# Two decoder layers in one launch: gates and one gelu written through tanh

## The chip, the cores and the metric

The kernel runs on one core of one Trainium2 chip. The metric is the device time of one execution in microseconds. Three executions of the kernel before took 1547.25, 1549.53 and 1549.8 us; the median is 1549.53 us. In the text PE is TensorE, DVE is VectorE, ACT is ScalarE, POOL is GpSimd and SP is SyncE, which here only starts DMAs.

## The reference, cut to what matters

288 rows (256 of a prompt and 8 x 4 of samples) pass two layers with shared weights. Each layer is a half-step SwiGLU, a mixer, and a second half-step SwiGLU. The mixer is what changes:

```python
h = _rmsnorm(x, p['g_mix'])
u, v, q, k, vv, qi, ki, wi, ga, gb = jnp.split(h @ p['w_in'], SPLIT_POINTS, axis=-1)
u = jax.nn.gelu(u)                       # the tanh form is jax's default
v = _rmsnorm(jax.nn.gelu(v), p['g_v'])
...
sv, attn = mixer(v, q, k, vv, qi, ki, wi)
merged = sigmoid(ga) * ((u * sv) @ p['w_pa']) + sigmoid(gb) * (attn @ p['w_pb'])
x = x + merged @ p['w_out']
```

`sv` is a causal 128x128 mix of `v` per channel group plus a bias. `attn` is attention over keys that an indexer chose: 64 of the prompt's own keys, or 256 out of 2052 for a sample, whose keys and values lie in a paged cache. All is fp32.

## The kernel before, in words

The residual `x` stays in on-chip memory, transposed, as eight blocks of 128 features by 288 rows. All large products are *units* (`add_unit`): one weight tile of 128x1024 fp32 (512 KB) gives one PSUM tile `mm` of 128x288. To keep fp32 precision in the PE's fp32r mode, weights and activations are each split in a rounded high part and a low rest: `wh`, `wl` (`unit_split`, lines 487 to 506: ACT copies `raw` to `wh`, DVE subtracts to get `wl`) and blocks `b` by `Pair.add` and `Pair.put` (lines 582 to 597). A unit then is 8 times 3 matmuls: high x high, high x low, low x high. That makes 9840 matmuls into `mm`. The `raw` tiles have four buffers and are loaded by DMAs that ACT's queue starts once a split is written; the three `mm` tiles rotate.

A mixer has, in order, units for the index key and weight, `qi`, `q`, `k`, `v` of the attention, `v` of the gating, seven of `gb`, eight of `u`, then eight times a `ga` unit and a `w_pa` unit, the last `gb`, eight of `w_pb` and eight of `w_out`. Each ends in an evacuation (`ev_u`, `ev_ga`, ...), a generator that issues the ACT and DVE work on the PSUM tile. `ta`, `tb` and `tc` are scratch tiles with two buffers each.

Between the units the sparse attention runs as generators (`sample`, `sample_qk`, `two_heads`, `attend`, ...): small matmuls into PSUM tiles `s`, softmax on ACT (tiles `lg` for the prompt, `lgs` for the samples, both with `AF.Exp`) and DVE. The samples' paged keys (`in_kT`) and values (`in_cv`) come through four 1 MB tiles named `ring`: SP starts eight DMAs of 128 KB for each tile (`loader`, lines 681 to 710), and two tiles at a time are multiplied (`s<-ring,qz` for keys, `s<-ring,b` for values).

The order on each engine is fixed when the program is built. Every instruction passes through `Engine.__getattr__` (line 294, which is why nearly all rows carry that line), which adds an estimated duration to a model clock of that engine. Generators give up their turn until the model says their operands are there (`ready`, `go`), and PSUM tiles of the attention are granted by the same clocks. So a changed estimate changes the order. For ACT the model adds 1283 ns when an activation needs another table than the last one (`TABLES`, line 218); activations that are not in `TABLES` never change the model's table. The actual `ACT_TABLE_LOAD` instructions are put in by the compiler.

Of the kernel before, what the change touches and what calls it, by code (L numbers as in the profile page):

```python
# [9 lines left out]
F32 = mybir.dt.float32  # L10
# [3 lines left out]
AF = mybir.ActivationFunctionType  # L14
OP = mybir.AluOpType
# [14 lines left out]
T = SEQ + DB * DT  # L30
# [11 lines left out]
LW = 2052  # L42
NB = 67
RING = 4

O_ID, O_SW, O_SEL = 0, 128, 256
O_CM, O_WSM, O_WSS, O_WM, O_MN, O_HM, O_ER = 384, 768, 896, 928, 992, 1056, 1064
# [167 lines left out]


class Engine:
    TABLES = {AF.Exp: "exp", AF.Silu: "silu", AF.Gelu_apprx_tanh: "gelu", AF.Sigmoid: "sigmoid"}

    def __init__(self, clocks, name, engine):  # L220
        self.c, self.n, self.e, self.table, self.mode = clocks, name, engine, None, None
# [1 line left out]
    def cost(self, k, a, kw):  # L223
# [33 lines left out]
        if self.n == "S":  # L257
            psum = str(getattr(a[1], "space", "")).endswith("PSUM")
            w = (51 if psum else 93) + 0.833 * n + 93 * ("accum_out" in kw)
            w += 94 * (hasattr(kw.get("scale"), "ap") + hasattr(kw.get("bias"), "ap"))  # L260
            t = self.TABLES.get(a[2])
            if t and t != self.table:
# [42 lines left out]
def trunk(ctx, tc, A, OUT):  # L305
    nc = tc.nc
    V, S, P, Q, PE = nc.vector, nc.scalar, nc.gpsimd, nc.sync, nc.tensor
    clocks = Clocks()
    clk = clocks.t
    V, S, P, Q, PE = (Engine(clocks, n, e) for n, e in (("V", V), ("S", S), ("P", P), ("Q", Q), ("PE", PE)))  # L310
# [4 lines left out]
    hlp = ctx.enter_context(tc.tile_pool(name="hlp", bufs=3))  # L315
    rgp = ctx.enter_context(tc.tile_pool(name="rgp", bufs=RING))
    tp = ctx.enter_context(tc.tile_pool(name="tp", bufs=2))
# [21 lines left out]
    x = cp.tile([128, KT, T], F32, name="x")  # L339
# [51 lines left out]
    def spawn_front(g):  # L391
        gens.insert(0, ((-1, 1e9), g))
# [11 lines left out]
    def go(eng, *aps):  # L404

        for _ in range(PRM["turn_n"]):
            if hurry[0] or clocks.after(aps, by=eng) <= max(clk["PE"], clk[eng]) and clk[eng] <= clk["PE"] + PRM["turn"]:
                return
            yield
# [124 lines left out]
    def sumsq(n, src):  # L534
        while squares[0] != n:
            yield
        if n == 0:
            S.activation(acc[:, :T], src, AF.Square)
        else:
            q = tp.tile([128, T], F32, tag="sq", name="sq")  # L540
            S.activation(q, src, AF.Square)
            yield from go("V", q)
            V.tensor_tensor(acc[:, :T], acc[:, :T], q, op=OP.add)
        squares[0] = (n + 1) % KT
# [13 lines left out]
    def rms_gen(key, full=True):  # L558
        yield from ready(acc)
        ps, tag = yield from palloc()  # L560
        sums(ps, acc)
        rs = mp.tile([128, 3], F32, tag="rs", name="rs", bufs=2)
        ms = mp.tile([128, 3], F32, tag="ms", name="ms", bufs=2)
        V.tensor_scalar(ms, ps[:, :3], 1.0 / D, EPS, op0=OP.mult, op1=OP.add)
        pfree(tag)
        P.tensor_tensor(rs, ms, mhalf.to_broadcast([128, 3]), op=OP.pow)
        yield from ready(rs)
        ps, tag = yield from palloc()
        c0 = 0 if full else 256
        spread(ps, lambda j: rs[:, j:j + 1], full)  # L570
        rb = mp.tile([128, T], F32, tag="rb", name="rb", bufs=2)
        copy(rb[:, c0:], ps[:, c0:T])
        pfree(tag)
        rstd_now[key] = (rb, rs)

    class Pair:
# [11 lines left out]
            V.scalar_tensor_tensor(lo.t, t, g, h.t.bitcast(F32), op0=OP.mult, op1=OP.subtract)  # L588
            self.h[n], self.l[n] = h, lo

        def put(self, n, t):
            h, lo = Block(F32R), Block(F32R)
            yield from go("S", t)
            S.activation(h.t, t, AF.Copy)
            yield from go("V", h.t)
            V.tensor_tensor(lo.t, t, h.t.bitcast(F32), op=OP.subtract)
            self.h[n], self.l[n] = h, lo

        def __call__(self, k):
# [81 lines left out]
    def loader():  # L681
        yield from wait("idx")
        n = 0
        for key in want:
# [4 lines left out]
            else:  # L689
                while n - state["used"] >= RING:  # L690
                    yield
# [21 lines left out]
    def mixer(l, xp, key, nxt, next_gain, next_rms):  # L713
        M = {"q": [], "sq": [], "qi": [], "vg": {}, "sv": {}, "ma": {}, "sb": {}}
        xs, a_, t_, m_ = Pair(), Pair(), Pair(), Pair()
# [88 lines left out]
        def ev_u(n):  # L804
            def ev(ps):
                t = tp.tile([128, T], F32, tag="ta", name="ta")
                S.activation(t, ps[:, :T], AF.Gelu_apprx_tanh)
                yield from go("V", t)
                V.tensor_tensor(t, t, M["sv"][n].t, op=OP.mult)
                M["sv"][n].free()  # L810
                yield from a_.put(n, t)
            return ev

        def ev_ga(n):
            def ev(ps):
                t = M["sa", n] = tp.tile([128, T], F32, tag="ta", name="ta")
                S.activation(t, ps[:, :T], AF.Sigmoid)
                yield
            return ev

        def ev_pa(n):
            def ev(ps):
                b = Block()
                M["ma"][n] = b
                V.tensor_tensor(b.t, ps[:, :T], M.pop(("sa", n)), op=OP.mult)
                yield
            return ev

        def ev_gb(n):
            def ev(ps):  # L830
                b = Block()
                M["sb"][n] = b
                S.activation(b.t, ps[:, :T], AF.Sigmoid)
                yield
            return ev

        def ev_pb(n):
            def ev(ps):
                t = tp.tile([128, T], F32, tag="ta", name="ta")
                V.tensor_tensor(t, ps[:, :T], M["sb"][n].t, op=OP.mult)  # L840
                m = tp.tile([128, T], F32, tag="tb", name="tb")
                V.tensor_tensor(m, t, M["ma"][n].t, op=OP.add)
                M["sb"][n].free()
                M["ma"][n].free()
                yield from m_.put(n, m)
            return ev

        def ev_out(n):
            def ev(ps):
                V.tensor_tensor(x[:, n], ps[:, :T], x[:, n], op=OP.add)  # L850
                yield from nxt.add(n, next_gain(n))
                yield from sumsq(n, x[:, n])
                if n == KT - 1:
                    spawn_front(rms_gen(next_rms))
            return ev
# [6 lines left out]
        for nm in PRM["order"].split() + ["gb", "u"]:  # L862
            n, ev = evs_[nm]
# [725 lines left out]
    def idle(what):  # L1589
        n = 0  # L1590
        while not what():
            hurry[0] = True
            if n > 4:
                clk["PE"] += 200
            hook()
            evacs(True)
            n += 1
            assert n < 1000
        hurry[0] = False
        return n  # L1600
# [8 lines left out]
    for i, u in enumerate(units):  # L1609
# [3 lines left out]
        n = idle(lambda: u["need"] is None or u["need"] in flags)  # L1613
# [84 lines left out]
```

## Time and profile before

| | |
|---|---|
| median of three executions | 1549.53 us |
| the profiled execution | 1547.6 us |
| its span, first to last instruction | 1545.8 us |
| PE busy | 1515.0 us, 98% |
| DVE busy | 976.0 us, 63% |
| ACT busy | 768.6 us, 50%, of it 69.3 us in 54 table loads |
| moved by DMA | 299.75 MB, mean 194 GB/s |

A row of a group of instructions reads: line, engine, operation, tiles written <- tiles read, shape, count, then busy us and mean ns of one, then the idle time of the engine right before them and what ended it. PE's instructions overlap: a 128x288 matmul is shown with some 295 ns, but they start 0.13 us apart. A PE that is busy 98% has little time to give back: the 1.8 us between the span and the execution's time lie outside the program.

### The profile page before, as it was taken

The numbers are of one execution on the slowest core, as the hardware profiler recorded it, in microseconds if no ns is written. First come the engines' busy times: TensorE is split into PE (matmuls) and PEld (weight loads), VectorE is DVE, ScalarE is ACT, GpSimd is POOL, SyncE is SP. The second block draws the span as 40 slices with busy tenths as digits, with TensorE's granted clock in tenths as the row PEclk, the third lists the DMA queues.
The fourth block names the chain that finished last, engine by engine and source line by source line (L and its number), as shares of the span: only waits on it lengthen the run. The fifth ranks groups of instructions, "written<-read, shape, count | busy, mean of one in ns | idle before, by whom it ended". The sixth has DMA issues, their size and how long they took to land.

```text
span 1545.8 us, 32344 instructions
## 1 busy us (share of the span) xinstructions
PE 1515.0 (98%) x12110; PEld 1444.6 (93%) x12110; DVE 976.0 (63%) x1987; ACT 768.6 (50%) x1241; POOL 52.5 (3%) x65
## 2 busy tenths in 40 slices
PE   8999999999999999999999999999999999999999
PEld 7999998987879999999999999989887799999999
DVE  6666558875554666665556665588855547666643
ACT  5444444657773454444444444446578634544432
POOL 1000011100000000000000000201000000000000
PEclk9999999999999999999999999999999999999999
DMA  7666555587887665545545555556888854454563
GB/s 256 213 206 192 174 156 161 179 268 239 261 273 232 209 191 194 166 165 164 168 158 167 171 159 162 155 165 191 272 250 276 278 176 164 162 166 164 162 181 112
DMA packets 162558, 299.75 MB, mean 194 GB/s; under 512 B 21857, under 2 KB 108386, under 8 KB 162402
## 3 DMA queue, kind: packets, MB, share of 16 engines
q10 hardware_dynamic: 61552, 212.95, 43.0%
q1 hardware_dynamic: 100850, 84.73, 18.0%
q8 instruction: 97, 1.59, 0.4%
q14 instruction: 59, 0.48, 0.1%
HBM read 294.83 MB, written 2.77 MB: 193 GB/s over the span
## 4 chain that ended last, share of the span: by engine, by line
PE 77%; issue 14%; DMA 4%; ACT 2%; DVE 2%; SPq 1%; POOL 1%; POOLq 0%; DVEq 0%; ACTq 0%
PE mm L294 71%; PE s L294 6%; DMA raw<-in_win 1%; DMA ring<-in_kT 1%; DMA ring<-in_cv 1%; SPq L294 1%; ACT L294 1%; POOL rs L294 0%; DVE b L294 0%; DVE wl L294 0%; ACT b L294 0%; ACT wh L294 0%; DMA b<-in_ws 0%; DMA x<-in_x 0%; ACT lg L294 0%
## 5 line engine op out<-in xcount | busy, mean ns | idle before, releaser
L294 PE MATMUL mm<-b,wh 128*128 128x288 f32 x6560 | 1327.5, 298 | 4.8 <-DVE b L294 2.6
L294 PEld LDWEIGHTS mm<-b,wh 128*128 128x128 f32 x6560 | 1047.5, 188 | 24.4 <-issue 14.3
L294 PE MATMUL mm<-b,wl 128*128 128x288 f32 x3280 | 965.9, 294 | 2.3 <-DVE wl L294 1.6
L294 ACT ACTIVATE wh<-raw 128x1024 fp32r<-128x1024 f32 (+3 forms) x421 | 435.0, 1034 | 548.9 <-PE mm L294 538.9
L294 DVE TENSOR_TENSOR wl<-raw,wh 128x1024 fp32r<-128x1024 f32 (+3 forms) x421 | 503.2, 1197 | 264.4 <-ACT wh L294 259.7
L294 PEld LDWEIGHTS mm<-b,wl 128*128 128x128 f32 x3280 | 615.9, 188 | 3.5 <-DVE wl L294 3.5
L294 DVE TENSOR_TENSOR ta<-mm,rb 128x288 f32<-128x288 f32 x88 | 40.3, 458 | 55.6 <-PE mm L294 49.3
L294 ACT ACT_TABLE_LOAD x54 | 69.3, 1283 | 9.5 <-DMA ring<-in_cv 3.7
L294 DVE TENSOR_TENSOR tc<-mm,tb 128x288 f32<-128x288 f32 x88 | 40.3, 458 | 52.6 <-PE mm L294 52.2
L294 POOL TENSOR_TENSOR rs<-ms,mhalf 128x3 f32<-128x3 f32 x8 | 11.4, 1423 | 1111.2 <-DVE ms L294 1035.4
L294 DVE TENSOR_SCALAR_CACHE_REDUCE jk<-z,ci 128x513 bf16<-128x513 f32 x62 | 46.6, 751 | 2.2
L294 DVE TENSOR_TENSOR tb<-ta,rb 128x288 f32<-128x288 f32 x88 | 39.7, 452 | 4.9 <-ACT ta L294 4.9
L294 DVE TENSOR_TENSOR b<-tc,b 128x288 fp32r<-128x288 f32 x88 | 39.7, 451 | 0.0
L294 PE MATMUL s<-ring,qz 128*32 128x256 f32 x512 | 34.2, 383 | 4.4 <-DMA ring<-in_kT 4.4
L294 ACT ACTIVATE b<-tc 128x288 fp32r<-128x288 f32 x88 | 37.7, 429 | 1.5 <-DVE tc L294 1.0
L294 ACT ACTIVATE ta<-ta 128x288 f32<-128x288 f32 x88 | 37.8, 430 | 0.8 <-DVE ta L294 0.7
L294 ACT ACTIVATE jk<-z,ci 128x513 bf16<-128x513 f32 x30 | 21.8, 726 | 30.0 <-DVE ci L294 28.5
L294 PE MATMUL s<-ring,b 128*32 128x256 f32 x512 | 33.9, 382 | 2.5 <-DMA ring<-in_cv 2.5
L294 DVE SCALAR_TENSOR_TENSOR x<-mm,x 128x288 f32<-128x288 f32 x32 | 14.7, 458 | 31.4 <-PE mm L294 31.4
L294 PEld LDWEIGHTS s<-ring,qz 128*32 128x32 f32 x512 | 16.4, 109 | 16.5 <-issue 5.8
L294 PEld LDWEIGHTS s<-ring,b 128*32 128x32 f32 x512 | 16.7, 109 | 15.2 <-DMA ring<-in_cv 5.3
L294 ACT ACTIVATE b<-s 128x16 fp32r<-128x16 f32 (+2 forms) x62 | 16.4, 280 | 26.3 <-PE s L294 13.1
(193 smaller groups left out, 845.3 us busy)
## 6 DMA issues: line engine op xcount, KB each, us to landing
raw<-in_wup ACTq DMA_DIRECT2D x173, 512.0 KB, 3.5
raw<-in_win ACTq DMA_DIRECT2D x96, 512.0 KB, 4.3
ring<-in_kT SPq DMA_DIRECT2D x256, 128.0 KB, 3.3
ring<-in_cv SPq DMA_DIRECT2D x256, 128.0 KB, 4.0
raw<-in_wdn ACTq DMA_DIRECT2D x64, 448.0 KB, 3.3
raw<-in_wdn ACTq DMA_DIRECT2D x32, 512.0 KB, 3.5
raw<-in_wpa ACTq DMA_DIRECT2D x16, 512.0 KB, 4.2
raw<-in_wpb ACTq DMA_DIRECT2D x16, 512.0 KB, 3.7
```

The source lines that it names most:

```text
L294: r = f(*a, **kw)
```

## The change

The sigmoids become `0.5 * (1 + tanh(x/2))` and the gelu of `u` becomes `0.5 * u * (1 + tanh(...))`, with the polynomial inside written out on ACT (`Square`) and DVE. The factors 0.5 are not multiplied in on the spot: that of `u` goes into the split of `a` (`put(n, t, 0.5)`), those of the gates into the last addition to `x`. The gelu of `v` keeps its activation. `Sigmoid` leaves the model's `TABLES`; `Tanh` doesn't enter it.

```diff
+GELU = float(np.sqrt(2.0 / np.pi))
 class Engine:
-    TABLES = {AF.Exp: "exp", AF.Silu: "silu", AF.Gelu_apprx_tanh: "gelu", AF.Sigmoid: "sigmoid"}
+    TABLES = {AF.Exp: "exp", AF.Silu: "silu", AF.Gelu_apprx_tanh: "gelu"}
-        def put(self, n, t):
+        def put(self, n, t, half=None):
             h, lo = Block(F32R), Block(F32R)
             yield from go("S", t)
-            S.activation(h.t, t, AF.Copy)
+            kw = {} if half is None else dict(scale=half)
+            S.activation(h.t, t, AF.Copy, **kw)
             yield from go("V", h.t)
-            V.tensor_tensor(lo.t, t, h.t.bitcast(F32), op=OP.subtract)
+            if half is None:
+                V.tensor_tensor(lo.t, t, h.t.bitcast(F32), op=OP.subtract)
+            else:
+                V.scalar_tensor_tensor(lo.t, t, half, h.t.bitcast(F32), op0=OP.mult, op1=OP.subtract)
 # ev_u
-                S.activation(t, ps[:, :T], AF.Gelu_apprx_tanh)
+                y = M["sv"][n]
+                S.activation(t, ps[:, :T], AF.Square)
+                V.tensor_tensor(y.t, ps[:, :T], y.t, op=OP.mult)
                 yield from go("V", t)
-                V.tensor_tensor(t, t, M["sv"][n].t, op=OP.mult)
-                M["sv"][n].free()
-                yield from a_.put(n, t)
+                V.tensor_scalar(t, t, GELU * 0.044715, GELU, op0=OP.mult, op1=OP.add)
+                V.tensor_tensor(t, t, ps[:, :T], op=OP.mult)
+                yield from go("S", t)
+                S.activation(t, t, AF.Tanh)
+                yield from go("V", t)
+                V.scalar_tensor_tensor(t, t, 1.0, y.t, op0=OP.add, op1=OP.mult)
+                y.free()
+                yield from a_.put(n, t, 0.5)
 # ev_ga, ev_gb
-                S.activation(t, ps[:, :T], AF.Sigmoid)
+                S.activation(t, ps[:, :T], AF.Tanh, scale=0.5)
 # ev_pa, ev_pb
-                V.tensor_tensor(b.t, ps[:, :T], M.pop(("sa", n)), op=OP.mult)
+                V.scalar_tensor_tensor(b.t, M.pop(("sa", n)), 1.0, ps[:, :T], op0=OP.add, op1=OP.mult)
-                V.tensor_tensor(t, ps[:, :T], M["sb"][n].t, op=OP.mult)
+                V.scalar_tensor_tensor(t, M["sb"][n].t, 1.0, ps[:, :T], op0=OP.add, op1=OP.mult)
 # ev_out
-                V.tensor_tensor(x[:, n], ps[:, :T], x[:, n], op=OP.add)
+                V.scalar_tensor_tensor(x[:, n], ps[:, :T], 0.5, x[:, n], op0=OP.mult, op1=OP.add)
```

The program before holds 54 table loads, the changed one 8: one for ACT's first instruction and one for the first silu, then in each layer one for the gelu of `v`, one for the first softmax, whose table also serves the tanh that follows, and one for the silu of the second half-step. The rows of all other kinds keep their counts, but for those below and some small copies that the model gives to the other of ACT and DVE.

On ACT, in layer 0 where the samples' first softmax (`lgs`) falls between units of `gb` (`b<-mm`), the order before is:

```order
L294 ACT_TABLE_LOAD
L294 ACTIVATE lgs,se<-lgs,sst 128x512
L294 ACT_TABLE_LOAD
L294 ACTIVATE b_5343<-mm 128x288
L294 DMA raw<-in_win 128x1024
L294 ACTIVATE wh<-raw 128x1024
L294 ACTIVATE b_5403<-mm 128x288
L294 DMA raw<-in_win 128x1024
L294 ACT_TABLE_LOAD
L294 ACTIVATE lgs,se<-lgs,sst 128x512
L294 ACTIVATE wh<-raw 128x1024
```

and at the same place of the changed kernel:

```order
L295 ACTIVATE b_5303<-mm 128x288
L295 DMA raw<-in_win 128x1024
L295 ACTIVATE wh<-raw 128x1024
L295 DMA raw<-in_win 128x1024
L295 ACTIVATE lgs,se<-lgs,sst 128x512 x3
L295 ACTIVATE b_4975<-s_5399 128x256
L295 ACTIVATE b_5404<-mm 128x288
L295 ACTIVATE wh<-raw 128x1024
L295 ACTIVATE lg,st<-lg,st,rq 128x128
```

The loads are gone, and three softmax pieces that stood a unit apart stand together, ahead of the next unit's evacuation; the prompt heads' next softmax (`lg`) now follows the samples' first piece after two evacuations of `gb`, where five stood between.

On DVE, at the evacuation of the first `u` unit of layer 0 (`ta_5839` before, `ta_5989` after; `b3` is its block of `sv`), before, with the next unit's and two weight splits between:

```order
L294 TENSOR_TENSOR ta_5839<-ta_5839,b3_4872 128x288
L294 TENSOR_TENSOR wl_5799<-raw_5508,wh_5798 128x1024
L294 TENSOR_TENSOR ta_5881<-ta_5881,b18_4900 128x288
L294 TENSOR_TENSOR wl_5884<-raw_5623,wh_5883 128x1024
L294 TENSOR_TENSOR b55_5891<-ta_5839,b38_5890 128x288
```

and after:

```order
L295 TENSOR_TENSOR b3_4872<-mm_5880,b3_4872 128x288
L295 TENSOR_SCALAR ta_5989<-ta_5989 128x288
L295 TENSOR_TENSOR ta_5989<-ta_5989,mm_5880 128x288
L295 TENSOR_TENSOR wl_5995<-raw_5720,wh_5994 128x1024
L295 SCALAR_TENSOR_TENSOR ta_5989<-ta_5989,b3_4872 128x288
L295 TENSOR_TENSOR b18_4900<-mm_5997,b18_4900 128x288
L295 TENSOR_TENSOR b44_5849<-s3_6078,b19_5847 128x256
L295 SCALAR_TENSOR_TENSOR b21_6032<-ta_5989,b17_6031 128x288
```

Two instructions of a `u` unit have become five, and the next weight split stands between the one ahead of the tanh and the one behind it.

On PE, at the last pair of value tiles of layer 0 (`s_6385` and `s_6487`); the pair stands, before, behind the second of the eight products of the second `ga` unit:

```order
L294 MATMUL mm<-b_3084,wh 128x288
L294 MATMUL mm<-b_3085,wh 128x288
L294 MATMUL mm<-b_3084,wl 128x288
L294 MATMUL s_6385<-ring,b_6777 32x256 x8
L294 MATMUL s_6385<-ring,b_6778 32x256 x8
L294 MATMUL mm<-b_3155,wh 128x288
```

and after, behind the fourth product of the `w_pa` unit that follows (`b_6271` is the fourth block of `a`):

```order
L295 MATMUL mm<-b_6271,wh 128x288
L295 MATMUL mm<-b_6272,wh 128x288
L295 MATMUL mm<-b_6271,wl 128x288
L295 MATMUL s_6487<-ring,b_6851 32x256 x8
L295 MATMUL s_6487<-ring,b_6852 32x256 x8
L295 MATMUL mm<-b_6387,wh 128x288
```

Between the two places lie 6 products of the one unit and 4 of the other, 30 matmuls into `mm`. Counted in the same way, the first pair of value tiles stands 48 such matmuls earlier than before, so that the eight pairs of a layer are spread over 408 matmuls into `mm` where it was 330. Layer 1 shows the same two moves. SP and POOL keep their instructions in their order.

## Rows read from the trace of the kernel before

**Rows 1.** The page: busy time, share and count of each engine.

```profile
PE 1515.0 (98%) x12110; PEld 1444.6 (93%) x12110; DVE 976.0 (63%) x1987; ACT 768.6 (50%) x1241; POOL 52.5 (3%) x65
```

**Rows 2.** Windows: length, then busy us of PE, PEld, DVE, ACT, POOL; PE clock; DMA.

```profile
300.00:320.00 20.00, 20.00 (x176) 18.90 (x173) 16.10 (x58) 13.52 (x26) 1.32 (x1) 1.00 0.87 276
353.00:474.00 121.00, 111.75 (x988) 95.16 (x987) 65.21 (x185) 87.06 (x160) 2.46 (x7) 0.99 0.84 262
440.00:460.00 20.00, 17.40 (x157) 14.44 (x156) 11.38 (x42) 15.68 (x43) 0.00 (x0) 0.91 0.84 265
483.00:544.00 61.00, 61.00 (x462) 61.00 (x462) 37.06 (x56) 26.57 (x40) 0.00 (x0) 1.00 0.66 205
1120.00:1240.00 120.00, 112.72 (x1007) 96.09 (x1006) 66.52 (x192) 87.48 (x161) 2.47 (x7) 1.00 0.85 268
```

**Rows 3.** Groups of ACT in 357 to 483 us (24 loads; as many in 1120 to 1250).

```profile
L294 ACT ACT_TABLE_LOAD x24 | 30.8, 1283 | 2.2 <-DVE wl L294 1.0 <-DVE b L294 0.9
```

**Rows 4.** ACT in order of time: start us, length us, engine, operation.

```profile
410.62 1.28 ACT L294 ACT_TABLE_LOAD   x1
411.92 0.72 ACT L294 ACTIVATE lgs<-lgs,sst 128x512 f32<-128x512 f32 x1
...
412.75 1.28 ACT L294 ACT_TABLE_LOAD   x1
...
414.04 0.41 ACT L294 ACTIVATE ta<-mm 128x288 f32<-128x288 f32 x1
```

**Rows 5.** PE's waits in 353 to 483 us: us in total, times, longest.

```profile
PE s L294 <- DVE b L294: 2.6, 1, 2.6
PE s L294 <- DMA ring<-in_cv: 1.7, 1, 1.7
PE s L294 <- POOL b L294: 1.6, 2, 0.8
PE s L294 <- DMA ring<-in_kT: 0.8, 2, 0.6
```

**Rows 6.** PE's waits in 1120 to 1250 us.

```profile
PE s L294 <- DMA ring<-in_cv: 0.8, 2, 0.6
PE s L294 <- POOL b L294: 0.7, 1, 0.7
```

**Rows 7.** SP in order of time, from 353 and from 1140 us.

```profile
379.44 94.89 SPq L294 DMA_DIRECT2D ring<-in_cv  x128
...
1145.85 93.68 SPq L294 DMA_DIRECT2D ring<-in_cv  x128
```

**Rows 8.** SP's waits in 353 to 474 us.

```profile
SPq L294 <- DMA ring<-in_cv: 10.4, 9, 2.0
...
SPq L294 <- PE s L294: 1.2, 5, 0.3
```

**Rows 9.** DMA issues: KB each, median us from issue to landing.

```profile
ring<-in_cv SPq DMA_DIRECT2D x256, 128.0 KB, 4.0
```

**Rows 10.** PE in order of time, first and last value pair of layer 0, last of layer 1.

```profile
397.57 1.92 PE L294 MATMUL s<-ring,b 128*32 128x256 f32 x32
...
479.18 1.93 PE L294 MATMUL s<-ring,b 128*32 128x256 f32 x32
...
1244.11 1.93 PE L294 MATMUL s<-ring,b 128*32 128x256 f32 x32
```

**Rows 11.** Groups by form: count, busy us, mean ns, idle before and its enders.

```profile
L294 ACT ACTIVATE ta<-ta 128x288 f32<-128x288 f32 x88 | 37.8, 430 | 0.8 <-DVE ta L294 0.7
L294 DVE TENSOR_TENSOR ta<-ta,b 128x288 f32<-128x288 f32 x16 | 7.1, 452 | 10.8 <-ACT ta L294 10.8
L294 DVE SCALAR_TENSOR_TENSOR x<-mm,x 128x288 f32<-128x288 f32 x32 | 14.7, 458 | 31.4 <-PE mm L294 31.4
L294 DVE SCALAR_TENSOR_TENSOR b<-x,gns,b 128x288 fp32r<-128x288 f32 x48 | 25.9, 545 | 0.6 <-ACT b L294 0.6
L294 DVE TENSOR_SCALAR lg<-lg,st 128x256 f32<-128x256 f32 x14 | 4.9, 350 | 0.1
```

More of the change, by code (lines that the diff above doesn't have):

```diff
@@ L832, in ev @@
                 M["sb"][n] = b
-                S.activation(b.t, ps[:, :T], AF.Sigmoid)
+                S.activation(b.t, ps[:, :T], AF.Tanh, scale=0.5)
                 yield
```

## The prediction, made before the run

> **What bounds the kernel now.** I read the page's busy times first, then the windows, then ACT, PE and SP inside the stretches that stood out. PE is busy for 98% of the span [rows 1], so the change can only win what PE waits, not what ACT or DVE save. In the windows the reader is to compare stretches: behind the attention, from 483 us, PE is busy for all of 61 us and starts 462 matmuls, 0.132 us each; from 300 to 320 us it is busy throughout too, with 276 GB/s arriving. But from 353 to 474 us and from 1120 to 1240 us, where both layers run the sparse attention between the units of `gb`, `u`, `ga` and `w_pa`, PE is idle for 121.00 - 111.75 = 9.25 us and 120.00 - 112.72 = 7.28 us [rows 2]. ACT is at its busiest there, 87 of 121 us, and 24 table loads, 30.8 us, are a third of that [rows 3]. In one slice of layer 0, 440 to 460 us, the granted clock is 0.91 of full; 0.09 of 20 us is 1.8 us. Full is the 2.4 GHz level, the other one 1.2; PE is idle for 2.6 us of that slice [rows 2]. These 9.3 + 7.3 + 1.8 = 18.3 us are all that the change can give back in these stretches.
>
> What ended PE's waits says how much of it is ACT's and DVE's: the ring's DMAs ended 1.7 + 0.8 us in layer 0 and 0.8 us in layer 1, POOL's mask products 1.6 and 0.7 us [rows 5, 6]. That is 5.6 us. The rest of the 16.5 us, 10.9 us, was released by DVE or ACT, most of it in single waits for a DVE result that itself came behind a late ACT (the largest is 2.6 us [rows 5]).
>
> There is a second limit right beside PE. SP starts the 128 value DMAs of a layer without a pause, 94.89 and 93.68 us long [rows 7]; in layer 0's stretch it waited 1.2 us for PE to free a ring tile and 10.4 us for its own earlier transfers [rows 8]. So the value stream is not held up by PE; it runs at the pace of SP and the DMA, and PE follows it: the last DMA of layer 0 goes out at 379.4 + 94.9 = 474.3 us, lands 4.0 us later [rows 9], at 478.3 us, and the last pair of value matmuls starts at 479.18 us. For layer 1 it is 1145.9 + 93.7 + 4.0 = 1243.5 against 1244.11 us [rows 10]. The slack is 0.9 and 0.6 us.
>
> **The change part by part.** *Table loads.* 54 become 8: of 24 in each stretch one stays. That takes 46 x 1.283 = 59.0 us off ACT [rows 3]. Squares replace gelus one for one, and 16 tanh from on-chip memory come on top, 16 x 0.430 = 6.9 us [rows 11]. ACT loses 52 us, 26 in each stretch: 87 of 121 us busy becomes about 61. None of this is on the path by itself; it is worth what PE waited for.
>
> *DVE.* A `u` unit's two instructions (2 x 0.452) become five: the product from PSUM and the second one from PSUM at 0.458 each, the two with three operands at 0.458, the nearest row with constants only (0.545, with a column operand, is the upper bound, 0.45 the lower), and a one-operand instruction of 288 columns between nothing and the 0.458 of two operands, for which I take the 0.350 of 256 columns with a column operand [rows 11]. That is 2.18 - 0.90 = 1.28 us a unit, 10.2 us a layer. DVE is busy 65 of 121 us there [rows 2], so it has room; if that cover were gone (DVE behind all the time), the 10.2 us of each layer would be PE's.
>
> *The other evacuations.* `w_pa`, `w_pb` and `w_out` change a two-operand for a three-operand instruction on the same tiles: 0.458 in both forms, and the 545 ns row would make it at most 0.09 us x 48 = 4.2 us of DVE, in stretches where DVE is busy 37 of 61 us [rows 2, 11]. The scales of 0.5 are constants: I take nothing. Both ends lie beside PE: 0 on the path, at worst the 4.2 us.
>
> *The wait that is added.* Inside a `u` evacuation ACT's tanh waits for DVE's product and DVE's next step for the tanh. On ACT the split of the next weights, with the DMA that it starts, stands ahead of the tanh, and on DVE the subtraction of that split stands there too, so what queues behind the waiting tanh is only the split of `a` and the next unit's square. The PSUM tile is held for three steps more (square, one-operand step, product: about 1.2 us plus hand-overs); three `mm` tiles rotate, and a unit takes 24 x 0.132 = 3.2 us of PE at the least.
>
> *The order.* With the loads gone from its clock the planner issues the softmax pieces sooner. The first pair of value tiles moves 48 matmuls forward, so PE will arrive there before the data and wait. The last pair moves 30 matmuls back: 30 x 0.132 = 4.0 us of unit work is then done ahead of it that came behind it. SP's and POOL's orders stay, so nothing is moved past their queues; ACT's weight DMAs go out as soon as a split is written, which is earlier wherever a load stood in front of it.
>
> *The sum.* If the value stream ends when it does now, each layer gains the slack plus the 4.0 us: 0.9 + 4.0 + 0.6 + 4.0 = 9.5 us. If the stream keeps up with a faster PE, the gain is the 10.9 us of waits plus 1.8 us of clock = 12.7 us. The stream can quicken a little: SP waits 10.4 us for its own transfers, and 262 GB/s in layer 0's stretch is under the 276 GB/s that arrived at 300 us [rows 2, 8]; the bytes of 121 us at 276 GB/s take 115 us. I take 12 us. Against the profiled execution's 1547.6 us that is 1535.6; that execution lies 1.9 us under the median of 1549.53, so a median after is predicted at 1537.5 us. The forecast's own range is 6 to 15 us of gain, 1534.5 to 1543.5.
>
> *One rule against the row.* ACT's rows show the next activation 0.02 us after a load's end: 410.62 + 1.28 = 411.90, and 411.92 [rows 4]. The Trainium skill, "ScalarE: Activation LUTs", "What ACT_TABLE_LOAD costs", puts a drain of some 1.38 us beside the 1.283 us of the load, 2.66 us in all. The load's length agrees with the trace, the drain does not show. By the page 46 loads would be 122 us, the stretch would have been ACT's, and all of the 18.3 us would come back, which is the first rival's time.
>
> **The rivals.** *All of it, or more.* The DMA has room above what it moves, the ring's waits shrink as well, and no clock drop is left: 18.3 us, 1531 us. For it: the single slices go beyond 262 GB/s. Against it: SP's stream has no pause to fill and no slack behind it [rows 7, 10]. The Trainium skill, "DMA: Bandwidth & Descriptors", "Specifications", gives a core about 358 GB/s from memory; by it the stream would be no limit and this rival the likeliest. The trace shows 262 to 276 GB/s and DMA shares of 0.84 to 0.87 [rows 2], so I give it 12 in 100.
>
> *Little or nothing.* The stream gets slower, because the weights' DMAs, issued earlier, crowd the value tiles just where the first pairs are now wanted sooner; 5% of 94.9 + 93.7 us is 9.4 us and eats the gain. For it: SP waits for transfers already, and the DMA's share is 0.84 and 0.85 [rows 2, 8]. Against it: the bytes per unit are the same, and the later pairs are wanted later. The time is 1543.5 to 1551; 18 in 100, of which 8 are still faster by more than 0.2%.
>
> *Slower.* The `u` chain becomes the pace. `ta` has two buffers, and a unit now keeps its own from the square to the last subtraction: 0.41 + 0.35 + 0.46 + 0.43 + 0.46 + 0.43 + 0.46 = 3.0 us of bare work, plus hand-overs and a weight split of 1.2 us in each queue, some 6 us. Two buffers carry that as long as it stays below two units. With attention work between, a unit takes 5.9 us here (330 matmuls, 13.75 units, from 397.57 to 479.18 us [rows 10]), so the limit is near 12 us; it decides when ACT or DVE puts two splits and a softmax into one chain. If that happened in all 16 units by 1.5 us, 24 us would be lost against 12 won: 1561 us. 12 in 100; DVE's 55% is against it.
>
> That the change does not do what it says is excluded by the built program, which holds 8 loads.
>
> **How the numbers follow.** Forecast 58 in 100, all faster; the large gain 12; little or nothing 18 (8 faster, 10 the same); slower 12. Faster by over 0.2% (3.1 us, about what a measurement of this kernel can tell from no change): 0.78; the same 0.10; slower 0.12. The range reaches from the large gain with 2 us to spare, 1529, into the little gain, 1547; slower and part of "the same" are left out.
>
> **What would show it.** Eight table loads; ACT in the two stretches down by some 26 us each, DVE up by 10; PE idle there down from 9.3 and 7.3 us to 2 to 5 each, with `ring<-in_cv` as the first name in its waits, above all at the first pair of value tiles; the last pair in each layer right behind the last landing; the stretches behind it at 0.132 us a matmul as before. I would be wrong if SP's 128 DMAs took clearly less or more than 94 us, or if PE waited for `mm` tiles or for blocks of `a` around the `u` units.

## The result and the profile after

Four runs of the changed kernel took 1566.62 to 1575.69 us, median 1570.25; four of the kernel before had a median of 1549.66. The ratio is 1.0137 (95% interval 1.0111 to 1.0164): slower by 21 us, where the forecast was 12 us faster and its range ended at 1547. The profiled run of after took 1572.31 us with a span of 1570.4.

The page's busy line of after, which answers to [rows 1]:

```profile
PE 1531.6 (98%) x12110; PEld 1452.3 (92%) x12110; DVE 986.8 (63%) x2019; ACT 722.8 (46%) x1227; POOL 52.5 (3%) x65
```

ACT did lose 45.8 us, and PE still got 16.6 us longer with the same 12110 matmuls. Of the 24 table loads of a stretch one is left, as said ([rows 3]; groups of ACT, 357 to 500 us):

```profile
L295 ACT ACT_TABLE_LOAD x1 | 1.3, 1283 | 0.0
```

The windows of after (length, busy us and starts of PE, PEld, DVE, ACT, POOL, then PE's clock and DMA's share and GB/s), against [rows 2]:

```profile
353.00:474.00 121.00, 112.56 (x960) 94.50 (x959) 72.25 (x219) 63.70 (x156) 2.46 (x7) 0.97 0.79 244
500.00:560.00 60.00, 60.00 (x456) 60.00 (x454) 37.77 (x56) 27.49 (x40) 0.00 (x0) 1.00 0.68 207
1120.00:1240.00 120.00, 111.98 (x971) 95.37 (x972) 77.53 (x239) 66.00 (x161) 5.80 (x16) 0.99 0.80 246
```

ACT is down by 23 and 21 us, yet PE is idle for 8.4 and 8.0 us, not 2 to 5, and starts 28 and 36 matmuls fewer than in the same windows before. The DMA moves less, 244 and 246 GB/s for 262 and 268. Behind the attention a matmul takes 60 / 456 = 0.132 us as before.

SP's value DMAs in order of time, against [rows 7], and the last value matmuls of each layer on PE, against [rows 10] (in brackets the wait before them and what ended it):

```profile
388.55 104.56 SPq L295 DMA_DIRECT2D ring<-in_cv  x128
...
1162.83 106.92 SPq L295 DMA_DIRECT2D ring<-in_cv  x128
```

```profile
495.65 1.05 PE L295 MATMUL s<-ring,b 128*32 128x256 f32 x10 [2.12 <-DMA ring<-in_cv]
...
1273.59 1.05 PE L295 MATMUL s<-ring,b 128*32 128x256 f32 x10 [2.41 <-DMA ring<-in_cv]
```

The stream that was taken as fixed at 94.9 and 93.7 us is 9.7 and 13.2 us longer, and PE waits for it at the very end. What SP waited for in 353 to 500 us stands in the first rows (us, times, longest), against [rows 8]; what PE waited for there in the next, against [rows 5]:

```profile
SPq L295 <- DMA raw<-in_win: 25.8, 12, 5.5
SPq L295 <- DMA raw<-in_wpa: 3.3, 2, 1.8
...
SPq L295 <- DMA ring<-in_cv: 0.6, 1, 0.6
```

```profile
PE s L295 <- DMA ring<-in_cv: 8.7, 10, 2.4
PE s L295 <- POOL b L295: 2.8, 2, 1.4
```

Before, SP waited for its own transfers, and for weight tiles only 0.2 us in layer 0 (353 to 474 us) and 2.4 us in layer 1 (1120 to 1250 us). Now it waits for weight tiles (`raw`), which SP doesn't start and which no value DMA needs; from 1130 to 1280 us it is 22.8 and 2.5 us, and PE's wait for `ring<-in_cv` is 9.9 us there [rows 6].

Why it can wait for them is seen in the program. Each DMA counts its landing on a semaphore, a counter on which instructions can wait, and those of SP and ACT share eight, `DMAHW0` to `DMAHW7`, in turn, in the order in which the program issues them. A DMA first waits until the one before it on its semaphore has landed. These are one tile's eight value DMAs on SP, in after and in the fourth experiment below, where POOL starts the weights:

```
after                                             weights on POOL
DMA ring_6167<-in_cv [waits DMAHW7_49,PE_49]      DMA ring_6167<-in_cv [waits DMAHW4_49,PE_49]
DMA ring_6167<-in_cv [waits DMAHW0_49]            DMA ring_6167<-in_cv [waits DMAHW5_49]
DMA ring_6167<-in_cv [waits DMAHW1_49]            DMA ring_6167<-in_cv [waits DMAHW6_49]
DMA ring_6167<-in_cv [waits DMAHW2_49]            DMA ring_6167<-in_cv [waits DMAHW7_49]
DMA ring_6167<-in_cv [waits DMAHW4_49]            DMA ring_6167<-in_cv [waits DMAHW0_49]
DMA ring_6167<-in_cv [waits DMAHW5_49]            DMA ring_6167<-in_cv [waits DMAHW1_49]
DMA ring_6167<-in_cv [waits DMAHW6_49]            DMA ring_6167<-in_cv [waits DMAHW2_49]
DMA ring_6167<-in_cv [waits DMAHW7_49]            DMA ring_6167<-in_cv [waits DMAHW3_49]
```

On the left number 3 is missing: a weight DMA of ACT took that turn, and the value DMA that comes eight turns later can't start until it has landed.

The records of the DMA starts in the traces bear this out. In after all of SP's and ACT's count on one set of eight semaphores; with POOL starting the weights, POOL's count on eight others. In after a weight tile ended twelve waits among the 128 value DMAs of layer 0, 19.8 us in all, and twelve in layer 1, 19.9 us, and each of these value DMAs waited for the one semaphore on which that weight tile counts. One such case, on PE, ACT and SP in after (SP's row is from its waits in 446 to 453 us, the others are in order of time):

```profile
441.30 1.05 PE L295 MATMUL s<-ring,b 128*32 128x256 f32 x10 [2.37 <-DMA ring<-in_cv]
...
454.60 1.29 PE L295 MATMUL s<-ring,b 128*32 128x256 f32 x10 [0.80 <-DMA ring<-in_cv]
```

```profile
443.84 0.41 ACT L295 ACTIVATE ta<-mm 128x288 f32<-128x288 f32 x1 [5.22 <-PE mm L295]
444.14 1.05 ACT L295 ACTIVATE wh<-raw 128x1024 fp32r<-128x1024 f32 x1
445.10 0.17 ACT L295 ACTIVATE b<-s 128x16 fp32r<-128x16 f32 x1
...
448.06 0.18 ACT L295 ACTIVATE b<-s 128x16 fp32r<-128x16 f32 x1 [0.24 <-DVE b L295]
448.07 0.33 ACTq L295 DMA_DIRECT2D raw<-in_win  x1
```

```profile
SPq L295 <- DMA raw<-in_win: 3.8, 1, 3.8
```

PE waits 2.4 us for the ring in the middle of a unit, so that unit's evacuation on ACT waits 5.2 us; the split and eight small copies stand behind it, and only then, at 448.07, the next weight DMA. SP waits 3.8 us for it to land (the value DMA that waits has no other wait than that weight tile's semaphore), the ring comes late again, and PE waits again at 454.60. In this case the stream, PE and ACT hold each other up in a circle.

### The profile page after: what moved, and what is told of

Its sections match the earlier page's. It is cut to its first block, busy times and chain, and to the rows that moved or that the text cites. A ratio compares the mean times of both kernels' runs of the same rounds, so it can differ in the third digit from the quotient of the medians.

```text
span 1570.4 us, 32361 instructions
## 1 busy us (share of the span) xinstructions
PE 1531.6 (98%) x12110; PEld 1452.3 (92%) x12110; DVE 986.8 (63%) x2019; ACT 722.8 (46%) x1227; POOL 52.5 (3%) x65
## 4 chain that ended last, share of the span: by engine, by line
PE 76%; issue 14%; DMA 7%; DVE 1%; SPq 1%; ACT 1%; POOL 1%; POOLq 0%; ACTq 0%; DVEq 0%
PE mm L295 68%; PE s L295 7%; DMA raw<-in_win 2%; DMA ring<-in_cv 2%; DMA ring<-in_kT 1%; SPq L295 1%; DMA raw<-in_wpa 1%; POOL rs L295 0%; DMA raw<-in_wup 0%; DVE b L295 0%; DMA x<-in_x 0%; DMA b<-in_ws 0%; DVE lgs L295 0%; DVE lg L295 0%; DVE wl L295 0%
## 5 line engine op out<-in xcount | busy, mean ns | idle before, releaser
L295 PEld LDWEIGHTS mm<-b,wh 128*128 128x128 f32 x6560 | 1054.1, 189 | 22.8 <-issue 14.7
L295 PE MATMUL s<-ring,b 128*32 128x256 f32 x512 | 44.5, 386 | 18.7 <-DMA ring<-in_cv 18.6
L295 ACT ACTIVATE b<-s 128x16 fp32r<-128x16 f32 (+2 forms) x72 | 19.9, 294 | 62.7 <-PE s L295 50.0
L295 ACT ACTIVATE ta<-ta 128x288 f32<-128x288 f32 x104 | 44.9, 432 | 6.7 <-DVE ta L295 6.6
L295 DVE SCALAR_TENSOR_TENSOR x<-mm,x 128x288 f32<-128x288 f32 x48 | 22.0, 458 | 36.4 <-PE mm L295 36.4
L295 ACT ACTIVATE ta<-mm 128x288 f32<-128x288 f32 x32 | 13.1, 410 | 42.1 <-PE mm L295 33.1
```

The lines of the kernel that those rows point to most:

```text
L295: r = f(*a, **kw)
```

## The experiments

**One and two: the order, and the arithmetic.** The change takes loads away, adds work to `u` and moves the order. The first gives the model back a table for tanh, so that the order is nearly that of before with 8 loads; the second keeps before's operations (32 loads) with the model's prices of the change, so that the order is nearly that of after.

```diff
# e1, in after
-    TABLES = {AF.Exp: "exp", AF.Silu: "silu", AF.Gelu_apprx_tanh: "gelu"}
+    TABLES = {AF.Exp: "exp", AF.Silu: "silu", AF.Gelu_apprx_tanh: "gelu", AF.Tanh: "tanh"}
# e2, in before
-    TABLES = {AF.Exp: "exp", AF.Silu: "silu", AF.Gelu_apprx_tanh: "gelu", AF.Sigmoid: "sigmoid"}
+    TABLES = {AF.Exp: "exp", AF.Silu: "silu"}
```

> The changed kernel, but the planner's table list also has Tanh, as a table of its own, so that it charges 1283 ns at each switch between softmax and gates as it did before; the program still holds 8 loads. Of the eight value pairs of layer 0 the first four stand, in units, at 98.5, 99.4, 102.1 and 102.5 (before: 98.5, 99.4, 102.2, 104.1; changed: 96.5, 98.1, 100.2, 102.6). Theory A (the loss comes from the order that the planner makes without the charge: ring tiles and weight DMAs interleave so that SP, which may only start a DMA when the one eight DMAs earlier in the program has landed, waits for ACT's weight DMAs): SP waits under 10 us per layer for raw tiles, the stretch's PE idle falls to 8 us a layer or less, time 1535 to 1550 us. Theory B (the longer evacuation of u and the added DVE work set the pace): the work is the same, so 1563 to 1575 us.

> The kernel before (sigmoid and gelu as single activations), but the planner charges no table load for gelu and sigmoid; the value pairs of layer 0 then stand at 96.4, 98.1, 100.0, 102.6, 105.5, 108.1, 110.9, 113.6 units, as in the changed kernel; the program holds 32 loads. Theory A: the order alone makes it slow, 1562 to 1580 us, with SP waiting 20 us or more per layer for raw tiles and PE for ring<-in_cv. Theory B: no added work, so 1543 to 1553 us.

The first took 1584.66 us (ratio 1.0211, 1.018 to 1.0243), the second 1559.53 (1.0063, 1.0042 to 1.0085). Each lies outside the ranges of both its theories. So after's order, without its arithmetic, costs some 8 us, but putting the order back makes the change worse, not better: the order alone isn't the cause. SP waited for weights in both. The rows of its waits in 353 to 500 us, first of the first and then of the second kernel:

```profile
SPq L295 <- DMA raw<-in_win: 19.2, 8, 4.9
SPq L295 <- DMA raw<-in_wpa: 6.4, 4, 3.5
```

```profile
SPq L294 <- DMA raw<-in_win: 18.5, 9, 4.5
SPq L294 <- DMA raw<-in_wpa: 2.9, 2, 1.5
```

**Three: the weights off ACT's queue.** POOL starts the weight tiles of 128 columns; its DMAs count on semaphores of their own.

```diff
-            (S if i > 2 else Q).dma_start(v, u["src"])
+            ((P if u["m"] == 128 else S) if i > 2 else Q).dma_start(v, u["src"])
```

> The changed kernel, but POOL and not ACT starts the weight DMAs, through a queue of its own, so that ring DMAs no longer stand behind weight DMAs in the turn of eight; the value pairs stand at 96.9, 98.5, 100.2, 103.0, 105.9, 108.4, 111.1, 113.9. Theory A with the weight DMAs as the cause of SP's waits: SP no longer waits for raw tiles, its 128 value DMAs take 95 us or less (105 and 107 in the changed kernel), PE waits for ring<-in_cv under 4 us (18.6), time 1540 to 1556 us unless POOL is too slow at starting transfers of 512 KB. Theory B: no change, 1563 to 1575. Theory C (the DMA's bandwidth, with the weights coming sooner, is what slows the ring): SP's value DMAs still take over 100 us, 1560 to 1575.

1522.29 us, ratio 0.981 (0.9786 to 0.9835): 48 us below the changed kernel with its `u` chain, its arithmetic and its bytes untouched, and below even the range of Theory A; its marks came: no wait of SP for weights in the stretches, value DMAs of 88.25 and 92.53 us, PE's wait for `ring<-in_cv` at most 0.5 us in each. That ends the `u` chain and the lack of DMA bandwidth as causes of the loss. But ACT's price in the model is gone too, and the order differs a little.

**Four, five and six: the same move with the order held.** The model goes on charging ACT, so each engine keeps its order; done to after, to before and to the first experiment.

```diff
+    W = Engine(clocks, "S", P)
-            (S if i > 2 else Q).dma_start(v, u["src"])
+            ((W if u["m"] == 128 else S) if i > 2 else Q).dma_start(v, u["src"])
```

> The changed kernel; POOL instead of ACT starts the weight tiles of the long units, and the planner goes on charging ACT's clock for it, so that every engine keeps the changed kernel's order. If the shared completion semaphores of SP's and ACT's DMAs are the loss: SP's 128 value DMAs within 97 us in each layer, none of SP's waits in the two stretches released by a weight DMA (25.8 and 22.8 us in the changed kernel), time 1515 to 1532 us. If the earlier POOL run won by its slightly other order instead: no more than 10 us below the changed kernel, 1560 to 1572 us.

> The kernel before with the same move: POOL starts the long units' weight tiles, the order on all engines is that of before, the 54 table loads stay. If the coupling only came into play with the change (before, SP waited for its own transfers alone): within 6 us of before, 1543 to 1551 us, and the changed arithmetic with POOL is then worth 15 to 25 us, its ACT savings being paid at last. If before was already held up by the coupling: 1525 to 1535 us, and the change is worth less than 10 us even without the coupling.

> The first experiment (changed arithmetic, tanh priced as a table of its own so that the order is nearly that of before, 8 loads; 1584.7 us) with POOL starting the long units' weight tiles and its order kept. If the coupling was the loss there too: SP's waits for weight tiles (21.6 and 22.5 us) gone, 1515 to 1535 us, 50 to 70 us below the same order with ACT starting them. If that order is bad by itself: it stays over 1550 us.

| median us | ACT starts weights | POOL starts weights | ratio to before, 95% |
|---|---|---|---|
| before | 1549.66 | 1527.85 | 0.9875 (0.9845 to 0.9904) |
| after | 1570.25 | 1521.23 | 0.9823 (0.9793 to 0.9852) |
| after, tanh priced | 1584.66 | 1541.35 | 0.9952 (0.9932 to 0.9973) |

The ratios are those of the POOL column, to runs of before made in the same round (median 1548.25), so the medians of the first column, from earlier rounds, give slightly other differences. The first line of the expectations for after holds: 49 us come back, all of it in the two mixers. From the first `s<-ring,qz` to the first `b<-tb` of ACT the timelines give, for layer 0 and 1, 224.6 and 220.1 us before, 233.4 and 232.6 after, 207.3 and 208.0 for after with POOL, 210.5 and 212.3 for before with POOL. Between the mixers, after takes 545.3 us with ACT and 545.6 with POOL.

After with POOL: SP's value DMAs, its waits in 353 to 500 us, and the window:

```profile
374.99 88.05 SPq L295 DMA_DIRECT2D ring<-in_cv  x128
...
1128.42 90.51 SPq L295 DMA_DIRECT2D ring<-in_cv  x128
```

```profile
SPq L295 <- DMA ring<-in_cv: 4.4, 7, 1.7
SPq L295 <- PE s L295: 1.5, 6, 0.4
```

```profile
353.00:474.00 121.00, 120.71 (x1118) 106.14 (x1118) 76.52 (x214) 68.06 (x163) 14.68 (x30) 1.00 0.89 283
```

No wait for weights is left, the stream takes 88 us, PE is busy 120.7 of 121 us and starts 1118 matmuls where after started 960; its clock is 1.00 there for after's 0.97, which is 3.6 us of the 121. So 94 us was not the pace of SP and the DMA. The 16.5 us by which the stream is shorter than in after are near the 19.8 us that its value DMAs waited there for weights.

Before with POOL falls in the second of its two expectations, that before was already held up by the coupling: 22 us down, 20 by the runs of its own round. All 24 loads of a stretch are still there; the group, PE's waits in 353 to 500 us, and the window:

```profile
L294 ACT ACT_TABLE_LOAD x24 | 30.8, 1283 | 1.3 <-DVE b L294 0.9
```

```profile
PE mm L294 <- DVE wl L294: 0.9, 2, 0.7
PE s L294 <- DMA ring<-in_cv: 0.4, 1, 0.4
PE s L294 <- PE s L294: 0.2, 1, 0.2
PE s L294 <- ACT pt L294: 0.2, 1, 0.2
```

```profile
353.00:474.00 121.00, 119.19 (x1085) 105.00 (x1080) 69.64 (x194) 91.50 (x171) 14.26 (x29) 1.00 0.86 276
```

With the loads kept, PE's idle time falls from 9.25 to 1.8 us. So the loads alone don't make the waits which the prediction put down to them. In before it was mostly ACT's weight DMAs that waited for SP's values. ACT's waits for `ring` in before, 353 to 482 us, none of which is there with POOL:

```profile
ACT pt L294 <- DMA ring<-in_cv: 3.3, 1, 3.3
...
ACT b L294 <- DMA ring<-in_cv: 1.9, 1, 1.9
ACT wh L294 <- DMA ring<-in_cv: 1.6, 1, 1.6
```

With POOL the change is worth 1527.85 - 1521.23 = 6.6 us, also under the 10 us of that expectation. The priced order lost 43 us to the coupling, less than the 50 that was expected; at 1541.35 us it lies between its two ranges, and it stays 20 us above after's own order with POOL; why is open.

**Seven: the weight DMA ahead of the split on ACT.** It then doesn't stand behind the split of its unit.

```diff
 def unit_split(i):
     u = units[i]
+    if i > 1:
+        unit_dma(i + 3)
 ...
     u["h"], u["l"] = h, lo
-    if i > 1:
-        unit_dma(i + 3)
```

> The changed kernel with ACT still starting the weight tiles, but ahead of the split of the unit three before instead of behind it, so that the DMA does not stand behind that split on ACT's queue; the planner's order moves with it. If the coupling is decided by what stands ahead of the weight DMA on ACT: SP's waits for weight tiles shrink from 25.8 and 22.8 us to under 15 us each and the time falls to 1535 to 1560 us, though ACT now waits for the raw tile's readers. If it doesn't matter where in ACT's queue it stands, since ACT's attention instructions hold it up either way: 1562 to 1580 us with SP's waits unchanged.

1628.74 us (1.0525, 1.0486 to 1.0564), far above both ranges. Its waits of ACT in 20 to 250 us tell why it answers another question:

```profile
ACT wh L295 <- DMA ring<-in_kidx: 35.8, 13, 3.2
ACT wh L295 <- DMA kx<-in_kidx: 13.4, 5, 3.5
```

In the same stretch of after the first row doesn't occur and the second is 0.2 us. Issued earlier in the program, the weight DMAs take other turns, and ACT now stands behind SP's index keys. It shows the coupling from ACT's side, not what was asked. SP's waits for weights came down somewhat and did not go: 16.0 us in 380 to 515 us and 15.6 in 1190 to 1300, around its value streams, above the 15 us of the first expectation.

**Eight: the weights on SP.** As in four, with `W = Engine(clocks, "S", Q)`.

> The changed kernel, SP instead of ACT starts the weight tiles of the long units, the order of all other instructions being the changed kernel's. ACT is relieved of the DMA starts as with POOL, but SP's value DMAs still stand behind weight DMAs, which now wait on SP itself for ACT's and DVE's split of the tile. If the loss is that the value stream is tied to ACT's progress: SP waits for ACT or DVE instead of for a weight tile, its 128 value DMAs take over 97 us in each layer, 1545 to 1600 us. If POOL's runs won because ACT's queue lost the DMA starts, or because the weights came sooner: 1515 to 1530 us.

1607.91 us (1.0383, 1.0354 to 1.0411), above both ranges. PE's largest wait of the whole span, and its wait for values in 353 to 540 us:

```profile
PE mm L295 <- ACT wh L295: 39.0, 7, 28.0
...
PE s L295 <- DMA ring<-in_cv: 1.1, 1, 1.1
```

Most of the loss sits outside the value stream. Of the 87 us above after with POOL, 43 lie ahead of the first mixer and 17 between the mixers: weights queue on SP behind other loads, and 31.6 of the 39.0 us fall in the first 170 us. In the stream PE hardly waits, and the eight pairs take 83.6 us (437.1 to 520.7) in layer 0 and 87.5 in layer 1, against 96.0 and 98.8 in after and 80.8 and 80.6 with POOL. SP's 128 value DMAs, with the weight DMAs between them, take 92.6 and 96.8 us, under the 97 that the first expectation set as the least, and their waits for weight tiles are 0.4 and 2.9 us. So weight DMAs that take turns with the stream cost it little when SP starts them itself; what cost it in after was that ACT's queue held them back. That ACT's relief is enough for the whole time is refuted.

**Nine: every second weight tile on POOL.**

```diff
-            ((W if u["m"] == 128 else S) if i > 2 else Q).dma_start(v, u["src"])
+            ((W if u["m"] == 128 and i % 2 else S) if i > 2 else Q).dma_start(v, u["src"])
```

> The changed kernel with every second weight tile of the long units started by POOL, the others by ACT as before, the order of all other instructions the changed kernel's. If each weight DMA of ACT costs the value stream its own wait: about half of the 49 us comes back, 1538 to 1556 us, with SP waiting 8 to 16 us for weight tiles in each stretch. If the loss feeds on itself (PE late, so ACT late, so the next weight tile late): more than two thirds come back, 1521 to 1537 us.

1559.37 us (1.0078, 1.0051 to 1.0106): 11 of 49 us, less than both expectations. The mixers take 232.1 and 220.9 us: layer 0 gains next to nothing against after, layer 1 gains 11.7 us, about half of the 24.6 between after and after with POOL. SP's waits in 353 to 500 us and in 1120 to 1310 us, and PE's in the first of these:

```profile
SPq L295 <- DMA raw<-in_win: 30.3, 10, 5.3
```

```profile
SPq L295 <- DMA raw<-in_wpa: 10.0, 5, 2.6
SPq L295 <- DMA raw<-in_win: 6.0, 4, 2.6
```

```profile
PE s L295 <- DMA ring<-in_cv: 7.9, 7, 1.9
```

In layer 0 half the weight DMAs make SP wait as long, 3.0 us each instead of 2.2; in layer 1 SP waits 16.0 us where it was 25.3. The streams take 99.65 and 99.77 us, between those of after and of after with POOL. So the price is not simply one per DMA, and neither expectation holds for both layers. That a single weight DMA, held back on ACT, stops the stream until ACT comes to it would fit layer 0, but is not shown.

## Why the prediction was wrong

*The loads and ACT: right in size.* 8 loads, ACT 45.8 us down for 52 predicted; 16 small instructions that the planner moved from DVE to ACT are the likely difference. The `u` unit's DVE work was well sized, by the rows of after in 400 to 480 us:

```profile
L295 DVE TENSOR_TENSOR b<-mm,b 128x288 f32<-128x288 f32 x8 | 3.6, 456 | 5.7 <-ACT ta L295 5.7
L295 DVE TENSOR_SCALAR ta<-ta 128x288 f32<-128x288 f32 x8 | 2.4, 300 | 0.0
L295 DVE SCALAR_TENSOR_TENSOR ta<-ta,b 128x288 f32<-128x288 f32 x8 | 3.6, 451 | 0.0
```

The one-operand step took 0.300 us for the 0.350 taken, the others 0.451 to 0.456 for 0.458; a unit has 2.11 - 0.90 = 1.21 us more, for 1.28 [rows 11].

*The step that failed: "the value stream is not held up by PE; it runs at the pace of SP and the DMA".* It rested on SP having no pause [rows 7] and waiting for its own transfers [rows 8]. But SP's row of 128 DMAs counts such waits as part of its length, and what it waited for was a turn of eight semaphores that ACT's weight DMAs share. The stream takes 88 us without that, 104.6 us with the change. The sum had the stream end when it did before, or sooner, and its lengthening at nothing; it became 9.7 and 13.2 us longer, and the mixers 8.8 and 12.5 us. The prediction's own mark, the 128 DMAs clearly off 94 us, is what came, on the side that no term of the sum had; of its other mark, waits of PE for `mm` or for blocks of `a`, there are 0.2 us in each layer's stretch.

*The step before it: "the rest of the 16.5 us, 10.9 us, was released by DVE or ACT".* As a reading it is 0.7 us too high, since the ring ended one more wait of PE in layer 0, beside those of [rows 5]:

```profile
PE mm L294 <- DMA ring<-in_kT: 0.7, 1, 0.7
```

As a cause it is wrong: in before with POOL the same loads leave 1.8 us idle. In layer 0 of before ACT itself waited 6.8 us at the starts of its weight DMAs for value tiles, and these waits are gone with POOL. The 18.3 us counted idle time and clock in two stretches only; after with POOL is 28 us below before, all of it in the two mixers.

*The step on the order: "nothing is moved past their queues; ACT's weight DMAs go out as soon as a split is written".* Each queue kept its order, but the turns run across SP and ACT together, and on ACT other evacuations stand between a split and its DMA, 2.9 us of copies in the case shown. The planner's clocks know nothing of the turns.

*The rivals.* "Slower" had its mechanism in the `u` chain; the chain was not it, since after with POOL keeps it and gains; that its 1561 us comes closest to the measured time is luck. "Little or nothing" came nearest in mechanism, with a stream slowed by weight DMAs, but by bandwidth; the stream slowed with less traffic, 244 for 262 GB/s.

What stays open: why one order is coupled harder than another (22, 49 and 43 us in the three lines of the table). That SP waits for the semaphores' turns is shown by the program and by the traces; that the turns alone, with ACT still starting the weights, make the whole 49 us is not, since no run has ACT start them on semaphores of their own.

## What to carry to other kernels

When a DMA queue waits, look at what its wait names: here a tile that the waiting transfer didn't need pointed to a shared semaphore, and it paid to keep long transfers that a busy engine starts late out of the turns of a stream on which PE depends. A queue that "never pauses" is not at its limit until its waits are counted out of its length. Before crediting an idle time to the instruction that ended it, ask what held that instruction up; here 22 us of the kernel before went with the loads untouched.

## What was not expected

The same DMAs with the same order took 49 us less of the kernel's time when another engine started them, though a weight tile from POOL's queue lands no sooner, and a value tile later (median 4.1 us for 3.3). The pages' DMA issues of after and of after with POOL (KB, median us to landing):

```profile
raw<-in_win ACTq DMA_DIRECT2D x96, 512.0 KB, 4.1
```

```profile
raw<-in_win POOLq DMA_DIRECT2D x96, 512.0 KB, 4.6
```

The Trainium skill, "DMA: Bandwidth & Descriptors", "Issuing engines are not separate DMA queues", says that starting DMAs from several engines saves only the sequencer's time to start them. For the transfer itself the rows agree; for the kernel the runs do not, because the starts wait for each other. DMA also went further than thought: 283 GB/s over the 121 us of layer 0's stretch, where before had 262.
